# A hybrid encoder layer on one core: six feature tiles by VectorE passes, conversions ahead of the modulated input, and another order of work where the feed-forward begins

## The chip, the core and the metric

The kernel runs on one core of a Trainium2 chip. The core has TensorE (PE: matmuls into PSUM), VectorE (DVE), ScalarE (ACT), GpSimd (POOL) and SyncE (SP), which here only issues loads. The metric is the device time of one execution in microseconds (us), the median of several runs. One measurement of this kernel is the profiled execution; all rows of a trace come from that one.

## The reference, cut to what matters

One layer on x of 256 x 2048, in float32, conditioned by a vector c:

```python
c_act = silu(c)
mod = c_act @ mod_w + mod_b                          # 2048 x 12288
sh_m, sc_m, g_m, sh_f, sc_f, g_f = split(mod, 6)
h = x * (1 + sc_m) + sh_m
y = attention(h @ w_qkv + b_qkv) @ w_o + b_o          # 32 heads of 64, 8 key heads, a band of 128, a sink
x = layer_norm(2**0.25 * x + (1 + g_m) * y) 
h = x * (1 + sc_f) + sh_f
y = square(relu(h @ w1 + b1)) @ w2 + b2               # 2048 -> 8192 -> 2048
x = layer_norm(2**0.25 * x + (1 + g_f) * y)
```

## The kernel before, in words

**Three products for one.** Each float32 operand is split into a rounded high half and a low half (what is left), and a product is the sum of high by high, high by low and low by high: three matmuls (`mm3`, L554 to L556; the feed-forward's own are L1045 to L1047, L1069 and L1070). The high half of a weight is a ScalarE conversion (`wh`, L288), the low half a VectorE subtraction (`wl`, L259).

**The stream of loads.** All weights come as 1 MB loads of 128 x 2048 (`raw`, L243), issued by SyncE in the order in which `S.plan` listed them, each as soon as a buffer is free. There are eight buffers in the first stage, five after it. A load is either a weight, which needs two conversions and two subtractions of 128 x 1024, or a piece of `mod_w`.

**The modulation, in two ways.** c times a piece of `mod_w` can be made by TensorE (`Mod.step`, L343: sixteen small matmuls per load, called product loads here), whose result is copied by ScalarE (L372) and turned to columns by one small matmul (`columns`, L423), or by VectorE (`Col.step`, L383): one pass over the whole load with c spread over the rows (`cb`, made by `spread`, L139), which gives one column. For the attention's scale and shift there is one group per feature tile of 128, two loads each. The table MIXP says which way: before, tiles 4, 8 and 12 go by VectorE passes, the other thirteen by TensorE. For the feed-forward there are four groups of four tiles, and FFP says how many tiles of each go by TensorE: 0, 4, 2 and 2.

**The units.** The first stage runs over twelve units. Each takes one load of `w_qkv`, that is four pairs (tile of 128 features, a third of the first 1536 outputs), of six matmuls of 128 x 512 each; in between come the feature loads (`S.vecs(1)`, letter g of the string `steps`) and `modulated(k)` (letter m): the turn to columns, x * scale + shift as a high half on ScalarE (L582) and a low half on VectorE (L583, L584). The bias of q, k and v is split into halves by `bias_rows` and added by a matmul at the end (L204). Before the units come dummy matmuls (`idle`, L647), twenty, six and six, that keep TensorE at work while the first loads arrive.

**Attention and its output.** The remaining q, k, v weights, the scores, softmax and output projection are woven by a written order of slots (`for n in range(OUT_AT + 16)`), with loads of the gates and of the feed-forward's modulation between them (SLOT_FILL). The last slot, `project` with `last` set, finishes the 128 rows of t = 0 first, and then those of t = 1; each is followed by the norm: `add_gated`, `norm_scalars` and `normed`.

**The handover.** After that, before, `ff_columns(0)` makes the first columns, and `S.vecs(4)` takes four loads of group 2. Then `ff_input(0)` transposes the normed tile (L975), modulates it (L981 to L989), and the feed-forward's first matmuls (L1045) begin with the weights `w1a`. Loads of groups 2 and 3 are spread over the first of the sixteen `w1a` steps (W1_FILL).

**Order.** The instructions of an engine run in a fixed order. A scheduler chooses it from what is written; `keep_in_program_order` and `S.pin` hold some of them in the written order.

## Time and profile before

| | us |
|---|---|
| median of 3 runs (lowest, highest) | 1123.53 (1122.96, 1123.92) |
| the profiled execution, its own time | 1121.65 |
| its span, first to last instruction | 1119.9 |
| TensorE busy | 1077.6 (96%) |
| VectorE busy | 747.6 (67%) |
| ScalarE busy | 527.0 (47%) |

The view of the stages gives the busy time of each engine in a stretch of the span. The list of waits says for whom an engine waited. A row of the timeline has the start in us, the duration in us, the engine, the line, the operation and what it writes and reads, with the count of instructions merged into it and, in brackets, the idle time before. A TensorE matmul of float32 operands shows as two records. A row of the groups has the busy time, the mean in ns of one, and the idle time before. In the view of one loading line, "to landing" is the time from issue to arrival.

### The profile page before, as it was taken

To read this page: it belongs to the slowest core of one execution; us is meant where nothing else is said; L and a number is where in the kernel's file an instruction comes from. 1 tells how busy PE (TensorE), PEld (TensorE's weight loads), DVE (VectorE), ACT (ScalarE), POOL (GpSimd) and SP (SyncE) were. 2 spreads that over 40 slices of the span, in tenths; PEclk is the share of its full clock that TensorE was granted. 3 is DMA by queue.
4 is the path that set the end of the run, shared out by engine and by line. 5 is a ranking of instruction groups with operands and counts; after the bars stand their busy time and mean duration, and the time that the engine had idled before them with its cause. 6 is when DMAs were issued, how large, how long until landed. Compare 5 with 4: busy or idle time off the path is not lost.

```text
span 1119.9 us, 16590 instructions
## 1 busy us (share of the span) xinstructions
PE 1077.6 (96%) x6712; PEld 886.7 (79%) x6712; DVE 747.6 (67%) x1086; ACT 527.0 (47%) x817; POOL 20.4 (2%) x40
## 2 busy tenths in 40 slices
PE   8888899999999799999999999999999999999995
PEld 5666676677778599988888888888888888888884
DVE  2455497889549875765577877766665656665576
ACT  2233357788753455654345543334444334444340
POOL 1000000000000000000000000000000000000001
PEclk9999999999999899999999999999999999999998
DMA  9999978888597878455678787876555555557521
GB/s 376 400 404 403 420 293 334 304 321 309 191 391 286 329 277 320 176 188 192 224 277 299 257 291 266 310 286 222 183 186 192 195 188 188 188 188 263 188 75 75
DMA packets 43797, 292.77 MB, mean 261 GB/s; under 512 B 5020, under 2 KB 5180, under 8 KB 9928
## 3 DMA queue, kind: packets, MB, share of 16 engines
q1 hardware_dynamic: 40400, 281.83, 67.5%
q0 software_dynamic: 2432, 8.41, 2.2%
q10 hardware_dynamic: 888, 1.48, 0.4%
q8 instruction: 52, 0.85, 0.3%
q14 instruction: 25, 0.20, 0.0%
HBM read 289.58 MB, written 2.11 MB: 260 GB/s over the span
## 4 chain that ended last, share of the span: by engine, by line
PE 89%; DVE 6%; ACT 2%; DMA 2%; issue 1%; DVEq 0%; ACTq 0%; SPq 0%
PE pa L1069 16%; PE pa L554 16%; PE pa L555 16%; PE pa L556 15%; PE pa L1070 8%; PE pm L343 4%; PE pa L1045 3%; PE pa L1046 3%; PE pa L1047 3%; DVE wl L259 2%; PE pa L735 1%; PE pa L793 1%; PE pt L777 1%; ACT wh L288 1%; DVE raw L383 1%
## 5 line engine op out<-in xcount | busy, mean ns | idle before, releaser
L259 DVE TENSOR_TENSOR wl<-raw,wh 128x1024 fp32r<-128x1024 f32 x332 | 403.1, 1222 | 232.6 <-ACT wh L288 229.3
L288 ACT CAST wh<-raw 128x1024 fp32r<-128x1024 f32 x332 | 346.4, 1051 | 410.5 <-PE pa L556 212.7
L555 PE MATMUL pa<-wl,g 128*128 128x512 f32 x816 | 320.9, 393 | 4.8 <-DVE wl L259 4.8
L554 PE MATMUL pa<-wh,g 128*128 128x512 f32 x816 | 316.5, 397 | 7.9 <-ACT wh L288 7.0
L556 PE MATMUL pa<-wh,g 128*128 128x512 f32 x816 | 318.8, 391 | 0.0
L1069 PE MATMUL pa<-g,wh 128*128 128x512 f32 x768 | 271.6, 399 | 0.0
L1070 PE MATMUL pa<-g,wl 128*128 128x256 f32 x768 | 215.7, 281 | 0.0
L554 PEld LDWEIGHTS pa<-wh,g 128*128 128x128 f32 x816 | 151.7, 188 | 48.6 <-ACT wh L288 11.3
L555 PEld LDWEIGHTS pa<-wl,g 128*128 128x128 f32 x816 | 153.5, 188 | 39.3 <-DVE wl L259 6.4
L556 PEld LDWEIGHTS pa<-wh,g 128*128 128x128 f32 x816 | 153.5, 188 | 33.1 <-issue 1.2
L1069 PEld LDWEIGHTS pa<-g,wh 128*128 128x128 f32 x768 | 144.3, 188 | 36.2 <-issue 0.2
L1070 PEld LDWEIGHTS pa<-g,wl 128*128 128x128 f32 x768 | 145.1, 189 | 0.1
L383 DVE CUSTOM_DVE_ANT_0 raw<-raw,cb 128x2048 f32<-128x2048 f32 x46 | 104.8, 2283 | 8.5 <-DMA raw<-in_mod 8.3
L1045 PE MATMUL pa<-g,wh 128*128 128x256 f32 x256 | 73.2, 287 | 0.0
L1046 PE MATMUL pa<-g,wh 128*128 128x256 f32 x256 | 72.9, 285 | 0.0
L1047 PE MATMUL pa<-g,wl 128*128 128x256 f32 x256 | 72.5, 283 | 0.0
L343 PE MATMUL pm<-raw,cact 128*32 128x128 f32 (+1 forms) x1344 | 54.6, 301 | 0.0
L343 PEld LDWEIGHTS pm<-raw,cact 128*32 128x32 f32 x1344 | 36.2, 111 | 18.6 <-issue 13.5
L1045 PEld LDWEIGHTS pa<-g,wh 128*128 128x128 f32 x256 | 49.1, 192 | 1.4 <-issue 0.9
L1046 PEld LDWEIGHTS pa<-g,wh 128*128 128x128 f32 x256 | 49.2, 192 | 0.5 <-DVE g L989 0.4
L1047 PEld LDWEIGHTS pa<-g,wl 128*128 128x128 f32 x256 | 49.2, 192 | 0.0
L436 DVE TENSOR_TENSOR modm<-pt,pack 128x2 f32<-128x2 f32 x13 | 2.1, 161 | 62.8 <-PE pt L423 62.7
(183 smaller groups left out, 697.3 us busy)
## 6 DMA issues: line engine op xcount, KB each, us to landing
raw<-in_mod SPq DMA_DIRECT2D x96, 1024.0 KB, 7.5
raw<-in_w SPq DMA_DIRECT2D x64, 1024.0 KB, 4.9
raw<-in_w1b SPq DMA_DIRECT2D x48, 1024.0 KB, 5.0
raw<-in_wqkv SPq DMA_DIRECT2D x24, 1024.0 KB, 8.3
raw<-in_wo SPq DMA_DIRECT2D x16, 1024.0 KB, 7.2
raw<-in_w1a SPq DMA_DIRECT2D x16, 1024.0 KB, 7.3
g<-in_x SPq DMA_DIRECT2D x4, 512.0 KB, 7.4
gb<-in_lnrow POOLq DMA_DIRECT2D x8, 256.0 KB, 5.7
```

The costliest lines, as they stand in the source:

```text
L259: self.pinned(nc.vector.tensor_sub(l, r, f32(self.hs[n])))
L288: self.pinned(nc.scalar.copy(h, s))
L343: i = nc.tensor.matmul(self.ps[32 * j:32 * j + 32, :w], lhsT[j] if type(lhsT) is list else lhsT, rhs[j], start=self.first, stop=stop)
L383: S.pinned(nc.vector.tensor_tensor_reduce(out=raw, in0=raw, in1=cb, scale=1.0, scalar=0.0, op0=OP.mult, op1=OP.add, accum_out=self.dst))
L554: nc.tensor.matmul(ps, xh, wh, start=start, stop=False)
L555: nc.tensor.matmul(ps, xh, wl, start=False, stop=False)
L556: S.prev = nc.tensor.matmul(ps, xl, wh, start=False, stop=stop).ins
L1045: nc.tensor.matmul(o, wh(w, 128), hh, start=new, stop=False)
L1046: nc.tensor.matmul(o, wh(w, 128), hl, start=False, stop=False)
L1047: nc.tensor.matmul(o, wl(w, 128), hh, start=False, stop=end)
L1069: nc.tensor.matmul(ps, wh(k, 128), hb, start=k == 0, stop=False)
L1070: nc.tensor.matmul(ps[:, :256], wl(k, 128), hb[:, :256], start=False, stop=k == NK - 1)
```

## The change

- MIXP: tiles 6, 10 and 14 go by VectorE passes too, so six tiles do. FFP: the feed-forward's groups have 0, 4, 4 and 0 tiles by TensorE; the number of product loads stays the same.
- The dummy matmuls multiply ones, made by VectorE alone, where they multiplied GpSimd's identity; there are 12, 5, 2 and 4 of them.
- The bias rows are loaded at the start, by GpSimd's queue, and the mask is made there; the bias split comes after unit 4, `spread` after unit 1, the rotary tables in units 5 to 9.
- The string of a unit gets a letter p, `S.pump(0)`: conversions of weights that have come, ahead of the unit's last `modulated`.
- In the last slot, the feed-forward's loads (four feature loads and the first weights) are written ahead of the norm of t = 1; `ff_columns(0)` comes in slot 19. The warming of the square root's table waits for the last softmax.

```diff
-MIXP = tuple(int(k not in (4, 8, 12)) for k in range(16))
+MIXP = tuple(int(k < 4 or k % 2) for k in range(16))
 FFG = (4, 4, 4, 4)
-FFP = (0, 4, 2, 2)
+FFP = (0, 4, 4, 0)
...
-    identr = cst.tile([128, 128], F32R, name="identr")
-    nc.vector.tensor_copy(identr, ident)
+    onesr = g4(F32R)[:, :128]
+    nc.vector.memset(ones := g4()[:, :128], 1.0)
+    nc.vector.tensor_copy(onesr, ones)
...
-            nc.scalar.dma_start(raw[p:p + m, :512], src.rearrange("o (m n) -> (o m) n", m=m))
+            nc.gpsimd.dma_start(raw[p:p + m, :512], src.rearrange("o (m n) -> (o m) n", m=m))
...
-        nc.vector.tensor_copy(hl, raw[:, :512])
-        nc.vector.tensor_sub(hl[32:32 + m], raw[32:32 + m, :512], f32(hl[32:32 + m]))
-        nc.scalar.copy(sel, one)
+        def split():
+            nc.vector.tensor_copy(hl, raw[:, :512])
+            nc.vector.tensor_sub(hl[32:32 + m], raw[32:32 + m, :512], f32(hl[32:32 + m]))
+            nc.scalar.copy(sel, one)
...
     load_x(0)
+    split_bias, bq = bias_rows(a["bqkv"], QKV)
+    msk = masks()
     S.pin = True
-    idle(20)
+    idle(12)
     S.vecs(1)
-    idle(6)
+    idle(5)
     S.vecs(1)
+    idle(2)
     modulated(0)
-    idle(6)
+    idle(4)
...
-        if n == 1:
-            steps = "ugugmugug"
+        if n == 0:
+            steps = "ugugmupu"
+        elif n == 1:
+            steps = "ugugmugugp"
         else:
-            steps = ["uuuu", "ugugumu", "ugugumgug"][len(ms)]
+            steps = ["uuuu", "ugugpumu", "ugugumgugp"][len(ms)]
...
+            elif x == "p":
+                S.pump(0)
...
-        if n == 0:
+        if n == 1:
             spread()
-            bq = bias_rows(a["bqkv"], QKV)
-        if n == 1:
-            msk = masks()
-        if 3 <= n < 8:
+        if n == 4:
+            split_bias()
+        if 5 <= n < 10:
             next(tables)
...
+        if n == 15:
+            warm = sml.tile([128, 4], F32, name="warm")
+            nc.scalar.activation(warm, rs, AF.Sqrt)
...
                 if t == 0:
                     yield
+                else:
+                    for _ in range(2 * len(js)):
+                        S.done(False)
+                    S.stop, S.behind, S.pin = 0, False, True
+                    S.nh = S.nl = 2
+                    S.pump(4, 2 * S.im + 2)
+                    S.nh, S.nl, S.pin = NHIGH, NLOW, False
                 add_gated(pss[t], t, c, g1, st)
...
-            for _ in range(2 * len(js)):
-                S.done(False)
...
-        if n == 16:
-            warm = sml.tile([128, 4], F32, name="warm")
-            nc.scalar.activation(warm, sums_of[0], AF.Sqrt)
...
+        if n == 19:
+            ff_columns(0)
...
-    S.behind = False
-    ff_columns(0)
-    S.stop = 0
-    S.vecs(4)
```

The order of instructions shows what this moves. ScalarE, the last three units; `mrow` is a copied product, `modm` marks the high half of a modulated tile, `wh` a converted weight half. Before:

```order
L372 COPY mrow<-pm 128x128
L288 CAST wh<-raw 128x1024 x2
L582 ACTIVATE g_1034<-g_824,modm 128x256
L372 COPY mrow<-pm 128x128
L582 ACTIVATE g_1034<-g_824,modm 128x256
L288 CAST wh<-raw 128x1024 x2
L372 COPY mrow<-pm 128x128
L582 ACTIVATE g_1034<-g_824,modm 128x256
L288 CAST wh<-raw 128x1024 x2
```

And in the changed kernel:

```order
L375 COPY mrow<-pm 128x128
L291 CAST wh<-raw 128x1024 x2
L585 ACTIVATE g_954<-g_772,modm 128x256
L291 CAST wh<-raw 128x1024 x2
L585 ACTIVATE g_954<-g_772,modm 128x256
L375 COPY mrow<-pm 128x128
L291 CAST wh<-raw 128x1024 x2
L585 ACTIVATE g_954<-g_772,modm 128x256
```

Before, each pair of conversions stands behind the modulated tile of its unit. Now tile 14 has no copy (it goes by VectorE), and conversions stand ahead of a modulated tile in each unit.

TensorE, from the end of the last projection on; `pm` is a product load's result, `pt` a transpose, L1045 and L1053 the feed-forward's matmuls. Before:

```order
L343 MATMUL pm<-raw,cact 32x128 x48
L975 MATMUL pt<-ident,g_2500 128x128 x8
L1045 MATMUL pa<-g_3505,wh 128x256
L343 MATMUL pm<-raw,cact 32x128 x13
L1046 MATMUL pa<-g_3505,wh 128x256
L1047 MATMUL pa<-g_3505,wl 128x256
L343 MATMUL pm<-raw,cact 32x128 x3
L1045 MATMUL pa<-g_3505,wh 128x256 x2
L1046 MATMUL pa<-g_3505,wh 128x256
L1047 MATMUL pa<-g_3505,wl 128x256
```

And in the changed kernel:

```order
L346 MATMUL pm<-raw,cact 32x256 x40
L983 MATMUL pt<-ident,g_2391 128x128 x8
L1053 MATMUL pa<-g_3411,wh 128x256
L1054 MATMUL pa<-g_3411,wh 128x256
L1053 MATMUL pa<-g_3411,wh 128x256
L1054 MATMUL pa<-g_3411,wh 128x256
L433 MATMUL pt<-ident,mrow 128x128
L1055 MATMUL pa<-g_3411,wl 128x256
L1053 MATMUL pa<-g_3411,wh 128x256
L433 MATMUL pt<-ident,mrow 128x128
L346 MATMUL pm<-raw,cact 32x256 x8
L1054 MATMUL pa<-g_3411,wh 128x256
```

Five product loads (40 matmuls) now stand ahead of the transposes, where three stood (48 matmuls, each half as wide), and a sixth stands behind the first six feed-forward matmuls.

SyncE's loads around the first feed-forward weights, with the engines that each waits for (the names of the queues apart, DVE or PE is the engine that frees the buffer). Before:

```order
L243 DMA raw<-in_mod 128x2048 [waits DMAHW0_49,DVE_49]
L243 DMA raw<-in_mod 128x2048 [waits DMAHW3_49,DVE_49]
L243 DMA raw<-in_mod 128x2048 [waits DMAHW4_49,DVE_49]
L243 DMA raw<-in_mod 128x2048 [waits DMAHW5_49,DMAHW2_49,DVE_49]
L243 DMA raw<-in_mod 128x2048 [waits DVE_49]
L243 DMA raw<-in_w1a 128x2048 [waits DMAHW6_49,DVE_49]
L243 DMA raw<-in_mod 128x2048 [waits DVE_49]
L243 DMA raw<-in_w1a 128x2048 [waits DMAHW4_49,DVE_49]
```

And in the changed kernel:

```order
L246 DMA raw<-in_mod 128x2048 [waits DMAHW6_49,DVE_49]
L246 DMA raw<-in_mod 128x2048 [waits DMAHW1_49,DVE_49]
L246 DMA raw<-in_mod 128x2048 [waits DMAHW2_49,DVE_49]
L246 DMA raw<-in_mod 128x2048 [waits DMAHW3_49,DVE_49]
L246 DMA raw<-in_mod 128x2048 [waits DMAHW4_49,DVE_49]
L246 DMA raw<-in_w1a 128x2048 [waits DMAHW5_49,PE_49]
L246 DMA raw<-in_mod 128x2048 [waits DMAHW6_49,PE_49]
L246 DMA raw<-in_w1a 128x2048 [waits DMAHW7_49,PE_49]
L246 DMA raw<-in_mod 128x2048 [waits DMAHW0_49,PE_49]
```

The load of the first `w1a` weights waited for VectorE before; it waits for TensorE now, as do the next four.

More of the change, by code (lines that the diff above doesn't have):

```diff
@@ L830, in normed @@
         if t:
[L831 removed]
+            tc.keep_in_program_order(nc.scalar.activation(z, z, AF.Identity, scale=rstd, bias=sc[2]))
         else:
[L833 removed]
+            tc.keep_in_program_order(nc.vector.tensor_scalar(z, z, mv[:, 0:1], rstd, op0=OP.subtract, op1=OP.mult))
     def project(js, c):
@@ L889, in project_0, with ff_columns @@
             nc.vector.scalar_tensor_tensor(z, z, ALPHA, y, op0=OP.mult, op1=OP.add)
+    a2 = cst.tile([128, NK], F32, name="a2")
+    b2 = cst.tile([128, NK], F32, name="b2")
+    def ff_columns(g):
+        m_ff[g].columns()
+        s = slice(4 * g, 4 * g + 4)
+        scf, shf = modf[:, 0], modf[:, 1]
+        nc.vector.tensor_mul(a2[:, s], lnT[:, 0, s], scf[:, s])
+        nc.vector.tensor_mul(b2[:, s], lnT[:, 1, s], scf[:, s])
+        nc.vector.tensor_add(b2[:, s], b2[:, s], shf[:, s])
     S.nh, S.nl = NHIGH, NLOW
```

17 lines of the change are left out of this document (2 added, 15 removed).

## The prediction

> **What bounds the kernel now.** First the page: the span, the busiest engine and the load rate in forty slices of 28 us.
>
> ```profile
> span 1119.9 us, 16590 instructions
> PE 1077.6 (96%) x6712; PEld 886.7 (79%) x6712; DVE 747.6 (67%) x1086; ACT 527.0 (47%) x817; POOL 20.4 (2%) x40
> GB/s 376 400 404 403 420 293 334 304 321 309 191 391 286 329 277 320 176 188 192 224 277 299 257 291 266 310 286 222 183 186 192 195 188 188 188 188 263 188 75 75
> ```
>
> TensorE is busy 96%, so only the 42 us in which it is not, and work taken off it, can give time. Loads run at 400 to 420 GB/s in the first five slices alone. Next the busy time by stage (stretch, length, then busy us of PE, PEld, DVE, ACT, POOL, clock, DMA share, GB/s); I cut at the first projection matmul, at the end of the first twelve units, at the end of the attention output, and where TensorE is last seen waiting.
>
> ```profile
> 17.70:141.80 124.10, 108.70 (x1122) 79.30 (x1126) 61.30 (x100) 40.27 (x64) 0.00 (x0) 0.99 1.00 407
> 141.80:375.00 233.20, 231.25 (x1490) 173.16 (x1482) 187.60 (x351) 152.46 (x331) 3.86 (x7) 1.00 0.79 299
> 375.00:388.60 13.60, 5.88 (x44) 3.78 (x44) 10.88 (x28) 8.05 (x14) 0.00 (x0) 0.62 0.99 398
> 388.60:1107.40 718.80, 718.80 (x3966) 620.97 (x3963) 477.28 (x584) 321.96 (x403) 9.74 (x16) 1.00 0.62 222
> 1107.40:1119.90 12.50, 0.09 (x1) 0.00 (x0) 8.55 (x16) 0.92 (x2) 1.74 (x1) 0.69 0.22 84
> ```
>
> TensorE idles 15.4 us in the twelve units, 7.7 us where the feed-forward begins, 12.5 us at the very end, and nowhere else by more than 2 us. The end is the same program before and after. So two places decide: the units, and the 13.6 us handover. What TensorE waited for (total, times, longest):
>
> ```profile
> PE pa L554 <- ACT wh L288: 7.0, 10, 1.0
> PE pa L555 <- DVE wl L259: 4.8, 4, 2.0
> PE pt L975 <- DVE g L833: 4.7, 1, 4.7
> PE pa L647 <- DVE identr L116: 4.1, 1, 4.1
> PE pt L975 <- ACT g L831: 3.1, 1, 3.1
> ```
>
> No load is in that list, though the DMA engines are full (share 1.00) in the units. The weights of the last unit show why: issue and landing from the view of the loading line, then ScalarE's conversion and the last bias matmuls.
>
> ```profile
> L243 SPq DMA_DIRECT2D raw<-in_wqkv x1: 384/384/384, 113.7 to 113.7; - x1
> DMA to landing us min/median/max: 10.2/10.2/10.2
> 133.46 1.98 ACT L288 CAST wh<-raw 128x1024 fp32r<-128x1024 f32 x2
> 141.24 0.45 PE pa L204 x2
> ```
>
> They landed at 123.9 and were first used at 133.46: the loads are 9.6 us ahead. In the units the chain through TensorE, ScalarE and VectorE is the bound, with the loads close behind.
>
> **Term 1, the start: 4.1 us earlier.** Rows of the start, and of the second feature load.
>
> ```profile
> 0.81 0.06 DVE L118 MEMSET eps<- 128x1 f32 x1 [0.81 <-PEq L1230]
> 3.49 0.56 DVE L116 CAST identr<-ident 128x128 fp32r<-128x128 f32 x1
> 4.11 7.38 PE L647 MATMUL pa<-identr 128*128 128x512 f32 x20 [4.11 <-DVE identr L116]
> 14.02 1.08 PE L343 MATMUL pm<-raw,cact 128*32 128x128 f32 x32
> L243 SPq DMA_DIRECT2D raw<-in_mod x1: 424/424/424, 1.7 to 1.7; - x1
> DMA to landing us min/median/max: 8.2/8.2/8.2
> ```
>
> The idle matmuls no longer wait for GpSimd's identity: a memset and a 0.56 us cast on VectorE, from 0.81, release them at about 1.6. Twelve at 7.38/20 = 0.37 us end near 6.0 (6.7 at the slow clock of the first dozen). The second feature load lands at 1.7 + 8.2 = 9.9; before, its product began at 14.02, behind the dummies, and now it can begin at 9.9. What follows is the same chain, so the first projection matmul comes about 4.1 us earlier. If fewer dummies leave the clock slow, some 1 us of this goes.
>
> **Term 2, the units.** Six feature loads (tiles 6, 10 and 14) go from TensorE to VectorE.
>
> ```profile
> L343 PE MATMUL pm<-raw,cact 128*32 128x128 f32 x768 | 26.4, 279 | 0.0
> L423 PE MATMUL pt<-both,mrow 128*128 128x2 f32 x24 | 4.2, 245 | 3.0 <-ACT mrow L372 2.9
> L383 DVE CUSTOM_DVE_ANT_0 raw<-raw,cb 128x2048 f32<-128x2048 f32 x6 | 13.5, 2285 | 0.0
> ```
>
> 24 loads cost TensorE 26.4 us, so six cost 6.6; three of twelve turns (4.2 us) cost 1.05. Together with the start, even if all 15.4 us of waits remain, the chain ends at 141.7 - 4.1 - 6.6 - 1.05 = 130.0. The conversions put ahead of the modulated input and the bias split put off can only take from those waits; I count on none of that, because now the loads bind. From 17.7 to 123.9 they came at 407 GB/s on average; without their breaks, which came when buffers were not freed, at the 420 of the fifth slice, the last unit's weights land 106.2 x (1 - 407/420) = 3.3 us earlier, at 120.6. From their conversion to the last bias matmul it took 141.7 - 133.5 = 8.2 us, so the end is 128.9 by the loads. Between 128.9 and 130.0 I take 129.5: **12.2 us earlier**, the start included. Bounds: 13.3 (conversion and matmuls a little faster) and 9 (waits grow).
>
> The Trainium skill, "DMA: Bandwidth & Descriptors", section "Where 436 GB/s comes from", says that for loads from HBM the HBM side binds, at some 358 GB/s. By it these 43.2 MB would land 14.5 us later than at 407, at 138.4, and the whole change would bring 3 us. The trace disagrees, with 400 to 420 in four slices.
>
> The extra passes add 6 x 2.285 = 13.7 us to VectorE's 61.3 in 124.1, some 75 of 116: the cover is its idle time. What queues behind a pass is the low half of the next weights, and TensorE waits for that; uncovered, each tile's pair (4.6 us) could push it back by some 2 us, 6 to 8 in all.
>
> A wait also has an after-effect.
>
> ```profile
> 40.62 0.79 PE L555 MATMUL pa<-wl,g 128*128 128x512 f32 x1 [2.01 <-DVE wl L259]
> 41.21 0.63 PE L556 MATMUL pa<-wh,g 128*128 128x512 f32 x1
> L556 PE MATMUL pa<-wh,g 128*128 128x512 f32 x816 | 318.8, 391 | 0.0
> ```
>
> After a wait of 2.01 us matmuls took 0.63, where the mean of all is 0.39. VectorE kept TensorE waiting there because the bias split, now put off, stood in its queue.
>
> The Trainium skill, "TensorE: Matmul & The Clock Gate", section "HAM oscillation", lets the clock fall only after a gap of over 3.4 us. The trace is stricter; by the page the short waits for loads to come would be harmless, by the row one in some units could cost up to 2 us, which the range takes in.
>
> The stage to 375.0 keeps TensorE at 231.25 of 233.2. It loses its lead in loads, but asks for 299 GB/s of 420, so I price that at 0, up to 2 us.
>
> **Term 3, the handover.** T is the end of the last projection matmul, 372.1 before. Rows of TensorE, VectorE, ScalarE and SyncE, and a load that has the queue to itself:
>
> ```profile
> 372.17 2.83 PE L343 MATMUL pm<-raw,cact 128*32 128x128 f32 x96
> 379.65 0.69 PE L975 MATMUL pt<-ident,g 128*128 128x128 f32 x2 [4.66 <-DVE g L833]
> 383.39 1.54 PE L975 MATMUL pt<-ident,g 128*128 128x128 f32 x6 [3.05 <-ACT g L831]
> 374.97 2.28 DVE L383 CUSTOM_DVE_ANT_0 raw<-raw,cb 128x2048 f32<-128x2048 f32 x1
> 362.28 0.33 SPq L243 DMA_DIRECT2D raw<-in_w1a  x1
> 370.24 2.00 ACT L288 CAST wh<-raw 128x1024 fp32r<-128x1024 f32 x2 [10.50 <-DMA raw<-in_w1a]
> L243 SPq DMA_DIRECT2D raw<-in_w1a x1: 328/328/328, 401.3 to 401.3; - x1
> DMA to landing us min/median/max: 5.0/5.0/5.0
> ```
>
> Before, VectorE did a 2.28 us pass and weight halves between the norm's small steps, and TensorE ran freely only from 388.6, T + 16.5. Now no pass stands there: group 2 is all products, and the norm's steps follow one another, so by their order the transposes are ready before the weights; that they are is the least certain part of this term and sets its lower bound. What is late next is a load. Five product loads fill all five buffers, and TensorE takes them only after T, at 2.83/3 = 0.94 each; SyncE can issue the first feed-forward weights at T + 1.1 (before: 362.28, T - 9.8), and they land at T + 6.1 (5.0 alone). The next load, 1 MB at 420 GB/s or 2.5 us later, is a product that stands ahead of nearly all feed-forward matmuls on TensorE: landing T + 8.6, done T + 9.7. From there TensorE is free: the second weights land at T + 11.1, and 42 matmuls of the first remain, at five per 0.6 us:
>
> ```profile
> 389.94 0.28 PE L1045 MATMUL pa<-g,wh 128*128 128x256 f32 x1
> 390.54 0.28 PE L1047 MATMUL pa<-g,wl 128*128 128x256 f32 x1
> ```
>
> that is 5.0 us, to T + 14.7. So 16.5 - 9.7 = 6.8 us; three product loads that came later are done (2.8); one that now comes before T takes back 0.9; a slow clock, as the 0.62 of that stretch, may take 1: **7.7 us**, with 3 and 10 as bounds.
>
> The square root's table load moves to an earlier place on ScalarE:
>
> ```profile
> 372.26 1.28 ACT L812 ACT_TABLE_LOAD   x1
> ```
>
> It hid before, since the first root came at 375; I price it at nothing, 1.3 us if it stood in the way where it is now.
>
> The sum: 12.2 + 7.7 = 19.9. The profiled execution took 1121.65 us, 1.75 beyond its span, and would take 1101.75; the median of the runs is 1.88 higher, so the forecast is **1103.6**.
>
> **The rivals.** *The handover gives nothing* (0.13): the first weights, issued 11 us later than before, or the product behind them, land 6 us after my T + 6.1, as the 10.2 above shows that loads can when others are queued. For: the order on SyncE. Against: the queue is then empty. Time 1103.6 + 6 = 1109.6. *VectorE becomes the bound in the units* (0.08): passes hold up the low halves, 6 to 8 us as worked out, 1110.6; against it, it idles half the stage. *Loads at the rate of the first slice, 376* (0.02): 43.2 MB take 114.9 us instead of 106.2, the end is 8.2 after 132.6, one term is gone but for 0.9, and the time 1115. *Slower* (0.05): TensorE, now waiting for loads in every unit, is granted half its clock. Its work after the start is 108.7 - 7.65 = 101 us; with a share f at half clock and 15.4 us of waits it ends at 13.6 + 101 (1 + f) + 15.4. It decides from f = 0.2, where this is 150.2, 20.7 after 129.5, and eats the gain; at f = 0.25 the time is 1129. For it: the 0.63 above. Against: one such stretch in 124 us before. That the change does not do what it says is excluded by the order of instructions.
>
> **How the numbers follow.** The forecast has 0.70. Its own range: 9 to 13.3 and 3 to 10 give 12 to 23.3 off, 1100 to 1111.5. The next two rivals fall into it, so 1099 to 1112 leaves out 0.1 to 0.15. About 0.2% (2 us) is what a measurement can tell from no change. Faster has 0.93 (forecast and three rivals), same 0.02 (several misses at once), slower 0.05.
>
> **What would show it.** First projection matmul near 13.6, waits for loads on TensorE in the units, last bias matmul near 129.5, then TensorE full until T near 361; weights issued 1 us after T and TensorE full from T + 9.7. I am wrong if the units end after 133, if the clock row shows 5 or 6 there, or if TensorE waits past T + 13.

## The result, and the profile after

The changed kernel took 1116.13 us (median of 5 runs, 1114.57 to 1117.61), the kernel before 1122.97 beside it (5 runs, 1121.1 to 1123.92). The ratio is 0.9939, with a 95% interval of 0.9923 to 0.9956: 6.8 us faster, where 19.9 were forecast. The forecast of 1103.6 and its range, 1099 to 1112, were too low: the fastest of the five runs took 1114.57.

The profiled execution took 1114.57 us, with a span of 1112.8. The stages of it (stretch, length, busy us of PE, PEld, DVE, ACT, POOL, clock, DMA share, GB/s), cut as for the kernel before: at the first projection matmul, at the last bias matmul of the units, at T, where TensorE runs freely again, and where its last work ends.

```profile
13.80:134.95 121.15, 103.14 (x924) 76.81 (x928) 73.84 (x111) 40.34 (x61) 0.00 (x0) 0.94 1.01 420
134.95:367.97 233.02, 229.48 (x1399) 170.92 (x1402) 180.69 (x348) 147.22 (x328) 3.77 (x7) 1.00 0.79 296
367.97:379.40 11.43, 9.60 (x114) 5.52 (x113) 8.31 (x22) 4.95 (x8) 0.00 (x0) 0.85 0.83 328
379.40:1100.30 720.90, 717.92 (x3866) 619.22 (x3862) 487.70 (x592) 326.11 (x409) 9.75 (x16) 1.00 0.64 227
```

Loads now run at 420 GB/s through the whole first stage, and still TensorE idles 18.0 us in it, more than the 15.4 before; its mean clock there is 0.94. In the fourth stretch it idles 3.0 us, where before it idled nowhere. The list of TensorE's waits names them (total, times, longest):

```profile
PE pa L558 <- DVE wl L262: 8.5, 5, 3.5
PE pa L557 <- ACT wh L291: 5.8, 6, 1.9
PE pa L1053 <- ACT wh L291: 4.5, 4, 2.4
PE pt L462 <- ACT mrow L460: 2.9, 1, 2.9
...
PE pm L346 <- DMA raw<-in_mod: 0.8, 2, 0.5
```

The largest sum is that for `wl`, the low halves of weights, 8.5 us (4.8 before), all of it in the units. Loads as the direct cause are 0.8 us; but ahead of its conversions ScalarE waited 11.2 us for loads of `w_qkv`, four times in the units, so a part of the waits for `wh` goes back to loads. Four pieces make up the span. The third ends at the first matmul of the fifteenth of the sixteen `w1a` weights (475.68 before, 467.62 after; the expectations below say "the last of the sixteen weights" for this mark).

| piece | before | by the prediction | after |
|---|---|---|---|
| start and units, to the last bias matmul | 141.69 | 129.5 | 134.95 |
| from there to T (with one product load more, 0.9) | 230.55 | 231.5 | 233.02 |
| T to the fifteenth `w1a` weights | 103.45 | 94.85 | 99.64 |
| from there to the end | 644.19 | 644.2 | 645.18 |
| span | 1119.9 | 1100.0 | 1112.8 |

So 5.4 us are missing in the units, 1.5 on the way to T, 4.8 in the handover and 1.0 behind it.

**Where the units lose it.** Rows of ScalarE, VectorE and TensorE in unit 6, whose modulated input is tile 10, one of the three new pass tiles, in order of time (start, duration, instruction, and in brackets the idle time before and what ended it):

```profile
76.51 2.00 ACT L291 CAST wh<-raw 128x1024 fp32r<-128x1024 f32 x2 [0.99 <-DMA raw<-in_wqkv]
...
77.59 1.22 DVE L262 TENSOR_TENSOR wl<-raw,wh 128x1024 fp32r<-128x1024 f32 x1 [1.44 <-ACT wh L291]
...
79.83 2.28 DVE L386 CUSTOM_DVE_ANT_0 raw<-raw,cb 128x2048 f32<-128x2048 f32 x1
...
82.04 2.29 DVE L386 CUSTOM_DVE_ANT_0 raw<-raw,cb 128x2048 f32<-128x2048 f32 x1
...
83.98 1.99 ACT L291 CAST wh<-raw 128x1024 fp32r<-128x1024 f32 x2 [4.97 <-DMA raw<-in_wqkv]
...
85.88 0.60 ACT L585 ACTIVATE g<-g,modm 128x256 fp32r<-128x256 f32 x1
...
86.51 0.41 DVE L586 TENSOR_SCALAR g<-g,modm 128x256 f32<-128x256 f32 x1 [1.97 <-ACT g L585]
...
88.05 2.35 DVE L262 TENSOR_TENSOR wl<-raw,wh 128x1024 fp32r<-128x1024 f32 x2
...
89.32 0.80 PE L558 MATMUL pa<-wl,g 128*128 128x512 f32 x1 [3.50 <-DVE wl L262]
89.91 0.63 PE L559 MATMUL pa<-wh,g 128*128 128x512 f32 x1
```

Both high halves of this unit's weights are ready at 78.51. One low half is made at 77.59; the other, ready to be made from 78.51, comes at 88.05. Ahead of it in VectorE's order stand the two passes, the low half of the modulated tile (L586, L587) and the first steps of the rotary tables (0.8 us, not shown); L586 waits for the modulated high half on ScalarE (85.88), and that stands behind the conversions of the next weights, put ahead of it by the letter p, which wait until 83.98 for their load. TensorE needs the low half at 85.82 and stands still for 3.50 us. Afterwards its matmuls take 0.63 us where 0.39 is the mean: the granted clock is 0.50 from 85.65 to 92.47.

**The handover.** T is 367.97, and the loads are as forecast, to 0.2 us: the first weights are issued at 369.03 (T + 1.1) and landed 4.8 us later. Rows of TensorE from there on:

```profile
367.90 4.52 PE L346 MATMUL pm<-raw,cact 128*32 128x256 f32 x80
...
375.06 0.38 PE L1053 MATMUL pa<-g,wh 128*128 128x256 f32 x1 [1.27 <-ACT wh L291]
...
377.58 1.84 PE L346 MATMUL pm<-raw,cact 128*32 128x256 f32 x16
...
430.08 0.39 PE L1053 MATMUL pa<-g,wh 128*128 128x256 f32 x1 [2.35 <-ACT wh L291]
```

The last product load takes 1.84 us instead of 0.94, and it begins at 377.58, 1.2 us after it landed (376.38): the first matmuls of the first weights stand ahead of it, which waited 1.27 and 0.45 us for their conversions and then ran at half clock. So TensorE is free at T + 11.4, not T + 9.7. And 60 us later it waits again, at the ninth weights, for 2.35 and then for 0.39 us: a wait that no step of the prediction had. Rows of VectorE and ScalarE ahead of it:

```profile
423.20 2.29 DVE L386 CUSTOM_DVE_ANT_0 raw<-raw,cb 128x2048 f32<-128x2048 f32 x1
...
425.93 1.02 ACT L989 ACTIVATE g<-pt,b,a 128x256 fp32r<-128x256 f32 x2 [4.78 <-DVE b L914]
...
429.00 1.98 ACT L291 CAST wh<-raw 128x1024 fp32r<-128x1024 f32 x2
```

The ninth weights had landed at 421.48. Their conversion stands behind the input of group 2 (L989) on ScalarE, which waits 4.78 us for the group's columns (`b`, L914); these stand behind a pass of group 3 on VectorE.

### The profile page after: what moved, and what is told of

Same layout as the page of the kernel before. It is cut to its first block, busy times and chain, and to the rows that moved or that the text cites. A ratio compares the mean times of both kernels' runs of the same rounds, so it can differ in the third digit from the quotient of the medians.

```text
span 1112.8 us, 15919 instructions
## 1 busy us (share of the span) xinstructions
PE 1071.0 (96%) x6377; PEld 880.0 (79%) x6377; DVE 761.2 (68%) x1098; ACT 522.9 (47%) x811; POOL 21.4 (2%) x42
## 3 DMA queue, kind: packets, MB, share of 16 engines
HBM read 289.58 MB, written 2.11 MB: 262 GB/s over the span
## 4 chain that ended last, share of the span: by engine, by line
PE 83%; DVE 8%; ACT 3%; DMA 3%; issue 2%; POOL 0%; SPq 0%; DVEq 0%; ACTq 0%; POOLq 0%
PE pa L1077 16%; PE pa L558 15%; PE pa L559 14%; PE pa L557 14%; PE pa L1078 8%; PE pm L346 3%; PE pa L1053 3%; DVE wl L262 3%; PE pa L1054 3%; PE pa L1055 3%; DVE raw L386 2%; DMA raw<-in_wqkv 1%; ACT wh L291 1%; PE pa L744 1%; PE pa L802 1%
## 5 line engine op out<-in xcount | busy, mean ns | idle before, releaser
L386 DVE CUSTOM_DVE_ANT_0 raw<-raw,cb 128x2048 f32<-128x2048 f32 x52 | 118.2, 2283 | 10.1 <-DMA raw<-in_mod 10.1
L1053 PE MATMUL pa<-g,wh 128*128 128x256 f32 x256 | 73.0, 288 | 4.5 <-ACT wh L291 4.5
L1053 PEld LDWEIGHTS pa<-g,wh 128*128 128x128 f32 x256 | 49.4, 194 | 5.4 <-ACT wh L291 5.4
L346 PE MATMUL pm<-raw,cact 128*32 128x128 f32 (+1 forms) x1024 | 47.0, 324 | 0.9 <-DMA raw<-in_mod 0.8
L346 PEld LDWEIGHTS pm<-raw,cact 128*32 128x32 f32 x1024 | 28.0, 112 | 19.4 <-issue 11.7
L761 ACT ACTIVATE g<-g,nm 128x256 f32<-128x256 f32 x64 | 31.8, 499 | 16.8 <-DVE nm L751 16.7
```

Of the source, the lines that this page charges most:

```text
L346: i = nc.tensor.matmul(self.ps[32 * j:32 * j + 32, :w], lhsT[j] if type(lhsT) is list else lhsT, rhs[j], start=self.first, stop=stop)
L386: S.pinned(nc.vector.tensor_tensor_reduce(out=raw, in0=raw, in1=cb, scale=1.0, scalar=0.0, op0=OP.mult, op1=OP.add, accum_out=self.dst))
L1053: nc.tensor.matmul(o, wh(w, 128), hh, start=new, stop=False)
```

## The experiments

All times are medians of 4 to 11 runs, against the kernel before on the same chip (1122.4 to 1123.2 us); the interval is that of the ratio to it.

### The low halves

Theory Q: in the in-order queues of ScalarE and VectorE the low half that TensorE needs next stands behind steps that it does not need. Its rivals are the loads, and the clock for a cause of its own.

**e1, a low half right behind its high half.** In the changed kernel a low half is written once the next high half is, or when its own unit begins.

```diff
-    if len(self.ls) < n - 1 and len(self.ls) - self.used < self.nl or ...
+    if len(self.ls) < n - (not self.pin) and len(self.ls) - self.used < self.nl or ...
```

> In the units a weight's second low half is written right behind its own high half, where the changed kernel writes it behind the next weight's first conversion. Nothing else differs. Theory Q (the in-order queues of ScalarE and VectorE hold up the low halves, and the waits halve the clock): TensorE's waits for wl in the units, 8.5 us in the changed kernel, fall below 3; the half-clock stretches, 13.65 us of the units there, fall to one of 3.4 or none; the units end near 130 instead of 134.6 and the time is about 1111.5. Rival L (the loads, or the time that TensorE itself needs, set the end): waits of about the same sum turn up on other tiles, the end stays at 134 to 135 and the time at 1116. Rival C (the half clock comes by itself and is no consequence of the waits): the waits go, the half-clock stretches stay, the end is near 132.

It took 1108.34 us, ratio 0.9864 (0.9850 to 0.9878): 7.8 less than the changed kernel by the medians. The profiled executions are 4.6 apart (here the slowest of four runs, there the fastest of five): 5.0 less in the units, 1.6 more on the way to T, where a half-clock stretch came at 202.3, 0.2 more in the handover, and 1.4 less behind it, where the edit changes nothing. The stage of its units, by the same view as above:

```profile
13.76:129.93 116.17, 102.64 (x924) 76.43 (x928) 73.46 (x110) 39.80 (x60) 0.00 (x0) 0.96 1.01 419
```

TensorE's waits in the whole of it:

```profile
PE pa L557 <- ACT wh L291: 6.4, 6, 1.8
...
PE pa L558 <- DVE wl L262: 4.3, 6, 1.9
```

And the timeline of VectorE in unit 6 and of ScalarE at the last unit's weights:

```profile
77.78 2.36 DVE L262 TENSOR_TENSOR wl<-raw,wh 128x1024 fp32r<-128x1024 f32 x2 [0.79 <-ACT wh L291]
...
80.84 2.28 DVE L386 CUSTOM_DVE_ANT_0 raw<-raw,cb 128x2048 f32<-128x2048 f32 x1
...
120.24 1.99 ACT L291 CAST wh<-raw 128x1024 fp32r<-128x1024 f32 x2
```

The units end at 129.93. TensorE idles 13.5 us instead of 18.0, and that is 4.5 of the 5.0 us; so the gain is in the waits, not in the clock, of which Q had expected more (the stretches at half clock are 10.2 us instead of 13.65, but the one that went was one in which TensorE stood still anyway); nor did the waits for `wl` fall below 3. The last weights, landed at 120.22, are converted at 120.24, those of the unit before, landed at 112.77, at 112.80, and ScalarE waits 14.5 us for loads ahead of its conversions: now the loads bind, as the prediction's term had it. In unit 6 both low halves are now made ahead of the passes, which are the same and as long.

**e2, without the letter p.**

```diff
-            steps = "ugugmupu"
+            steps = "ugugmuu"
...
-            steps = ["uuuu", "ugugpumu", "ugugumgugp"][len(ms)]
+            steps = ["uuuu", "ugugumu", "ugugumgug"][len(ms)]
```

> The changed kernel without the letter p: no conversions of weights ahead of the modulated input, all else as changed. Theory Q: ScalarE no longer waits for the next weights' load ahead of the high half of tiles 6, 10 and 14, so the high half and with it the low half come 1 to 2 us earlier there, but the second low half still stands behind the passes; the units end at 132 to 134 instead of 134.6, time 1113.5 to 1116. Rival P (the letter p is a gain, since it puts conversions earlier): waits for wh grow by a conversion and a modulated half in each of the ten units, about 1 us each, the end is near 140 and the time 1121.

1120.91 us, 0.9978 (0.9967 to 0.9988); the units end at 144.02. The rival was right: the waits for `wh` are 12.1 us, where they were 5.8. Q's picture was incomplete. Rows of ScalarE and VectorE in unit 6:

```profile
79.69 2.00 ACT L291 CAST wh<-raw 128x1024 fp32r<-128x1024 f32 x2
...
83.01 2.29 DVE L386 CUSTOM_DVE_ANT_0 raw<-raw,cb 128x2048 f32<-128x2048 f32 x1
...
88.39 0.41 DVE L586 TENSOR_SCALAR g<-g,modm 128x256 f32<-128x256 f32 x1 [0.67 <-ACT g L585]
...
89.93 3.49 DVE L262 TENSOR_TENSOR wl<-raw,wh 128x1024 fp32r<-128x1024 f32 x3
```

Both high halves of this unit's weights are ready at 81.69, but now both low halves, not only the second, stand behind the passes and the modulated tile 10. From its list of waits:

```profile
PE pa L558 <- DVE wl L262: 10.3, 4, 8.7
```

One wait has become 8.7 us long. The letter p is worth some 5 us to this change: it is the smaller of two evils.

**e4, without p and with the low halves at once.** Both edits above.

> The changed kernel without the letter p and with each low half written right behind its own high half. Theory Q: both causes of held-up halves are gone; at best the loads bind, W11's weights land near 120 and the units end at 128.9 to 130.5, time 1110 to 1112. If the letter p is needed (rival P), waits for wh take the place of those for wl and the end is at 134 or later, time 1116 or more.

1119.67 us, 0.9965 (0.9953 to 0.9977), units to 143.98: nearly the same as e2. In unit 9 the edit acts (the first low half comes 0.7 us behind its high half, 6.6 in e2), but not in unit 6: the high halves are ready at 81.87, the first low half again comes at 90.11, behind the passes, and TensorE waits 8.72 us for it. The waits for `wl` are 10.3 us as in e2, those for `wh` 11.4, so the time is the rival's, though one wait did not take the place of the other. Why the order in unit 6 stayed the traces do not show; what they show is that without p the edit of e1 gains nothing.

**e3, three tiles by passes instead of six.**

```diff
-MIXP = tuple(int(k < 4 or k % 2) for k in range(16))
+MIXP = tuple(int(k not in (4, 8, 12)) for k in range(16))
```

> The changed kernel with three feature tiles by VectorE passes as before (4, 8, 12) instead of six. TensorE gets the 6.6 us of product loads and 1.05 us of turns back. Theory Q (the passes are what holds up the low halves): of the 8.5 us of waits for wl and the 6.8 us that the half clock takes, about as much goes as TensorE gains work, and the units end at 133 to 136, the time is 1115 to 1118, so that the three further tiles bring nothing in the units. Rival (the passes cost nothing and TensorE's work counts in full): the end is near 142, the time 1124.

1114.81 us, 0.9931 (0.9917 to 0.9945), units to 134.54, where the changed kernel had 134.95; four kernels with the same units (the changed one, e8, e9 and e13) end them at 134.38 to 135.22. Their stage:

```profile
13.89:134.54 120.65, 108.57 (x1122) 79.67 (x1126) 60.83 (x99) 40.75 (x63) 0.00 (x0) 0.97 1.01 419
```

TensorE is busy 5.4 us longer (not 7.65, since in the changed kernel more of the work runs at half clock) and waits 5.9 less (12.1). So the three further tiles, 7.65 us of work by the prediction, bring nothing in the changed kernel: what they take off TensorE comes back as waits.

**e11, three tiles with the low halves at once.** The edits of e3 and e1.

> Three feature tiles by passes as before, with each low half right behind its high half. It tells what the three further tiles are worth once the low halves are not held up. If TensorE's 7.65 us count there: the units end 4 to 7.65 us later than with six tiles and the same order of halves (129.9), at 134 to 137.6, time 1112 to 1116. If the loads or the waits for high halves set the end: 130 to 131, time 1108 to 1109.

1109.33 us, 0.9894 (0.9871 to 0.9917), units to 131.78, 1.85 later than in e1. Their stage:

```profile
13.96:131.78 117.82, 107.05 (x1122) 77.88 (x1126) 60.60 (x98) 40.17 (x63) 0.00 (x0) 1.00 1.01 419
```

Of the 7.65 us only 1.85 is left, because with six tiles the loads bind and with three they do not: here ScalarE waits for no load ahead of a conversion, the last weights, landed at 120.02, are converted at 122.78, and TensorE works without a wait from 108 to the end of the units. It has more work but waits 10.8 us instead of 13.5, and none of it runs at half clock. In the time the two kernels cannot be told apart: this one's runs went from 1108.2 to 1116.7, with a mean clock from 0.995 down to 0.988, on which more at the end.

**e12, the kernel before with the low halves at once.** The edit of e1 in the kernel before.

> The kernel before, with each low half right behind its high half in the units. Its waits for wl there are 4.8 us in four places, with one half-clock stretch. Theory Q, if the held-up halves are old: 2 to 5 us faster than before, 1118 to 1121. If they are the change's own making (letter p and six tiles): within 1.5 us of before, 1121.5 to 1124.

1117.62 us, 0.9956 (0.9942 to 0.9969): 5 us by the ratio, of which its profiled execution, the slowest of its runs, shows 2.2. The held-up halves are older than the change; with it, by the medians, there is more to win from them (7.8). Rows of the kernel before, ahead of the wait of 2.01 us that the prediction shows:

```profile
26.25 1.98 ACT L288 CAST wh<-raw 128x1024 fp32r<-128x1024 f32 x2
...
36.56 0.16 DVE L436 TENSOR_TENSOR modm<-pt,pack 128x2 f32<-128x2 f32 x1 [8.03 <-PE pt L423]
...
39.34 1.23 DVE L259 TENSOR_TENSOR wl<-raw,wh 128x1024 fp32r<-128x1024 f32 x1
```

The low half could have been made from 28.23 and was made at 39.34. The bias split took 1.1 us of that on VectorE; for 8.03 us VectorE stood idle ahead of a step for the modulated tile, with the low half behind it in its order.

**e5, dummy matmuls in the two longest waits of the units.**

```diff
+FILL = {6: 20, 10: 8}
...
+            if i == 2:
+                for _ in range(FILL.get(n, 0)):
+                    tc.keep_in_program_order(nc.tensor.matmul(sums[p][0], zer, wh(i), start=False, stop=False))
```

> The changed kernel with dummy matmuls (zeros by a weight half, added to a sum that is open, so that nothing in the result changes) where TensorE waits longest: 20 in unit 6, ahead of its third pair, and 8 in unit 10. At 0.23 us each they fill 4.6 of the 5.4 us and 1.8 of the 2.3 us that TensorE idles there; the halves that it waits for come no earlier. Theory Q (a wait of some 2 us makes the clock fall to half for 3.4 us or a multiple): the half-clock stretches behind those two waits, 10.2 us together, go, the units end 4 to 5 us earlier, near 130, and the time is near 1111.5, although more is computed. Rival C (the half clock has another cause): the stretches stay, the end is at 135 to 136 and the time at 1116 to 1117.

1116.50 us, 0.9946 (0.9932 to 0.9959), units to 136.64. It tells little. The dummies of unit 10 ran at 125.67, 7 us behind the wait that they were meant for, which stayed at 2.26 us; those of unit 6 (4.8 us) left a wait of 2.56 there, since TensorE, at full clock where it had been at half, came to them earlier. Half-clock stretches followed both waits. So neither theory falls by it, though the time is C's.

### The two halves of the change

**e6, the units' part alone; e7, the handover's part alone.** In both, the diff of the change is split between `MIXP`, the start, the bias rows and `steps` on one side, and `FFP`, `warm`, `normed`, `project` and `ff_columns` on the other.

> The kernel before with the first half of the change alone (start, six feature tiles, letter p, bias split), without the other order where the feed-forward begins. By the terms of the prediction, 12.2 us: 1110.8. By what the trace of the changed kernel shows (units end 6.7 us earlier, 2 us of it given back before the feed-forward): 1117 to 1119.

> The kernel before with the second half of the change alone: the feed-forward's loads ahead of the norm of t = 1, the first columns in slot 19, group 2 all by TensorE and group 3 all by VectorE, the table's warming. By the prediction's term, 7.7 us: 1115.3. By the trace of the changed kernel (from the end of the projection to the last of the sixteen feed-forward weights 99.6 us instead of 103.5, less 0.9 for the product load that comes before it): 1119 to 1120.

e6 took 1118.16 us, 0.9966 (0.9953 to 0.9978); e7 1120.97, 0.9982 (0.9973 to 0.9991). Against the runs beside them (1122.56) that is 4.4 and 1.6 us, together 6.0, near the 6.8 of the whole: the halves do not disturb each other much. In e7 TensorE waited 3.01 us at the first `w1a` matmul, the weights landing 6.6 us after their issue instead of the 5.0 that were counted: 1.6 us of what the rival "the handover gives nothing" had named.

### The wait at the ninth weights

**e8, the passes of group 3 planned earlier.**

```diff
-    W1_FILL = [1, 1, 1, 0, 0, 2, 0, 3, 0, ...
+    W1_FILL = [1, 1, 1, 0, 0, 3, 0, 4, 0, ...
```

> The changed kernel with the eight pass loads of group 3 planned earlier by one or two places (W1_FILL 3 and 4 at the sixth and eighth weight instead of 2 and 3, none left for the ninth), so that the last two passes are written ahead of the columns of group 2. Theory Q: the last two passes no longer stand ahead of those columns on VectorE, ScalarE's conversion of the ninth weights no longer waits behind the group's input, and the wait of 2.35 and 0.39 us at 427.7 goes with the half-clock stretch of 3.4 us behind it: 4.4 us, time 1111.5 to 1113. Rival L (loads bind there: the sixth to eighth weights have 2.7 to 4.3 us to spare and come 2.5 us later each): waits of 1 to 4 us on those weights take its place, time 1115 to 1117.

1117.06 us, 0.9951 (0.9939 to 0.9963): nothing. The wait went from the ninth weights to the eighth, and grew. Rows of ScalarE and TensorE there:

```profile
422.27 1.02 ACT L989 ACTIVATE g<-pt,b,a 128x256 fp32r<-128x256 f32 x2 [0.25 <-DVE b L914]
...
425.34 1.98 ACT L291 CAST wh<-raw 128x1024 fp32r<-128x1024 f32 x2
...
426.43 0.58 PE L1053 MATMUL pa<-g,wh 128*128 128x256 f32 x1 [4.05 <-ACT wh L291]
```

The eighth weights had landed at 418.0; their conversion stood behind the input of group 2 (L989) on ScalarE. So the wait is as long as rival L had it, but the loads are not its cause.

**e9, the input of group 2 ahead of the sixth weights.**

```diff
-        if n in (1, 7, 9):
+        if n in (1, 5, 9):
```

> The changed kernel with the columns and the input of group 2 made ahead of the sixth feed-forward weights instead of the eighth (their product loads, all by TensorE now, are done at 379). Theory Q: these columns stood on VectorE behind passes of group 3, ScalarE's input of group 2 behind the columns, and the conversion of the ninth weights behind that input; with the columns ahead of the passes the wait of 2.74 us at 428 and the half-clock stretch behind it (1.7 us) go: from the end of the projection to the last of the sixteen weights 95 to 96 us instead of 99.6, time 1111.5 to 1112.5. Rival W (the wait only moves: the passes now come behind the columns, and the input of group 3 waits for them): one wait of 2 to 4 us elsewhere before the last of the sixteen weights, 98 us or more, time 1115 to 1116.

1113.83 us, 0.9921 (0.9908 to 0.9934), from T to the mark 98.8 instead of 99.6; against the changed kernel's 0.9939 (0.9923 to 0.9956) that is no clear gain. Rival W was nearer: the input is done by 417, and the ninth weights' conversion now stands behind another step, a copy of sums (L1059) that waits for TensorE. Rows of both:

```profile
427.73 0.58 ACT L1059 COPY g<-pa 128x512 f32<-128x512 f32 x1 [2.05 <-PE pa L1055]
428.21 4.83 ACT L291 CAST wh<-raw 128x1024 fp32r<-128x1024 f32 x5
...
429.31 0.38 PE L1053 MATMUL pa<-g,wh 128*128 128x256 f32 x1 [1.62 <-ACT wh L291]
```

**e10, e1 and e9 together.**

> The changed kernel with both edits: a low half right behind its high half in the units, and the input of group 2 ahead of the sixth weights. If the two held-up queues are all that was missing of the forecast, and are independent: 1108.3 less 4.4, that is 1104; the forecast was 1103.6. If a wait takes the place of the second: 1108.

1108.64 us, 0.9875 (0.9860 to 0.9889): no faster than e1 alone. T to the mark is 96.9 instead of 99.9, but the rest takes 646.2 instead of 643.8. Of these 2.4 us, 0.9 are matmuls that start late for `wl` between 680 and 710 (1.9 in all, 1.0 in e1), and 1.5 is the second block of the hidden layer, which takes 90.8 us in fourteen of the profiled executions and 89.4 in the other four, e1 among them, without a wait that shows. Why it does is open.

### The clock

**e13 to e16, dummy matmuls in the waits behind the units.** Ten ahead of the gate's transposes, five ahead of the first `w1a` matmul and ten ahead of the ninth weights' first matmul: in the changed kernel (e13), in e1 (e14), in e10 (e15) and in e11 (e16).

```diff
+    def fill(ps, n):
+        for _ in range(n):
+            tc.keep_in_program_order(nc.tensor.matmul(
+                ps, fil, fil[:, None, :].to_broadcast([128, 4, 128]), start=True, stop=True))
...
             nc.scalar.copy(r, m.ps[:, :256])
+            fill(pt, 10)
...
             ps = opened[fq, fp]
+            if fp == 0 and n in (0, 8):
+                fill(ps, 5 if n == 0 else 10)
```

> The changed kernel with dummy matmuls (into a bank that the next matmul overwrites) at the three places behind the units where TensorE waits: ten ahead of the gate's transposes (wait 2.94 us at 203), five ahead of the first feed-forward matmul (1.27 and 0.45 at 374), ten ahead of the ninth weights' first matmul (2.35 and 0.39 at 428). They fill 2.3, 1.2 and 2.3 us of the waits; what TensorE waits for comes no earlier. Theory G (the clock is set in a fixed grid of stretches of 3.41 us: one in which TensorE idles for half or more makes the next one run at half clock): no half-clock stretch behind these places any more; 3.4 us less than the profiled execution of the changed kernel, which had two of them, 4 us less in the median, whose runs also had one at 207: 1112 to 1113. Rival C (the clock has another cause, such as the load on TensorE before): the stretches stay, 1116.

> The same dummies in the kernel with each low half right behind its high half. That kernel's profiled execution had half-clock stretches at 202.3, 373.0 and 427.6, behind the units. Theory G: all three go, 5.1 us less than its 1108.3: 1103 to 1104.5. Rival C: 1108.

> The same dummies with both edits, the low halves and the input of group 2 ahead of the sixth weights. Theory G: two or three half-clock stretches go, 1103.5 to 1105.5 where it was 1108.6. Whether the early input of group 2 brings anything, now that its wait no longer costs clock: 0 to 1.5 us against the run without it.

> The same dummies with three feature tiles by passes and each low half right behind its high half. Its profiled execution had one half-clock stretch only, at 426.7, its runs 1108.2 to 1116.7. Theory G: 1.7 us less than the best of these or more, 1105 to 1107; against the run with six tiles and the same dummies it tells what three further tiles are worth: 1 to 2 us by the ends of the units, 131.8 and 129.9.

The view of the stages, cut at the clock's own grid of 3.41 us (busy TensorE is the first number behind the length, the clock the third from the end). In e1 2.51 of the 2.94 us of wait ahead of the gate's transposes fall into one stretch:

```profile
198.88:202.28 3.40, 0.89 (x8) 0.89 (x9) 3.40 (x9) 1.96 (x5) 0.00 (x0) 1.00 0.63 186
202.29:205.69 3.40, 3.40 (x18) 1.94 (x18) 2.92 (x3) 2.12 (x3) 0.00 (x0) 0.50 0.98 393
```

In the changed kernel the grid cuts the same wait in two, and at the ninth weights it does not:

```profile
201.71:205.11 3.40, 1.76 (x20) 0.71 (x18) 3.27 (x5) 2.72 (x6) 0.00 (x0) 1.00 0.53 219
205.12:208.52 3.40, 2.11 (x18) 1.70 (x20) 3.37 (x7) 2.44 (x7) 0.00 (x0) 1.00 0.93 318
208.53:211.93 3.40, 3.40 (x24) 2.25 (x21) 3.19 (x8) 1.69 (x3) 0.00 (x0) 1.00 0.97 342
...
426.99:430.39 3.40, 1.04 (x9) 0.83 (x7) 3.34 (x11) 2.29 (x4) 0.00 (x0) 1.00 1.01 410
430.40:433.80 3.40, 3.01 (x15) 2.77 (x14) 3.29 (x4) 3.40 (x6) 0.00 (x0) 0.50 0.85 284
```

With 0.89 or 1.04 us of work in a stretch the next one runs at 0.50; with 1.76 and 2.11 it does not. Where dummies fill the waits, at the gate's transposes in e14 (e1 with dummies) and at the ninth weights in e13:

```profile
197.99:201.39 3.40, 2.98 (x16) 2.04 (x13) 3.40 (x7) 2.72 (x7) 0.00 (x0) 1.00 0.49 118
201.41:204.81 3.40, 3.40 (x31) 2.37 (x31) 3.37 (x5) 2.13 (x4) 0.00 (x0) 1.00 0.90 376
...
427.51:430.91 3.40, 3.40 (x28) 3.31 (x28) 3.40 (x6) 2.22 (x5) 0.00 (x0) 1.00 1.01 378
430.92:434.32 3.40, 3.40 (x24) 3.07 (x23) 3.33 (x8) 3.40 (x5) 0.00 (x0) 1.00 1.00 369
```

At these two places, eight in the four kernels, no half-clock stretch is left; without the dummies the same four kernels had one at five of the eight. And no dummy brought forward what was waited for: the waits make the half clock, theory G. At the first `w1a` weights one stayed in each (two in e14), since there the wait went to the product load: 2.6 us, and 3.9 in e16.

The time followed only in part: none of the four lies where G had put it, and e14 is at rival C's 1108. e13: 1114.24 us, 0.9924 (0.9911 to 0.9938), 1.9 less than the changed kernel though the intervals overlap, and its runs lie within 0.8 us where the changed kernel's lie within 3.0. e14: 1108.12, 0.9873 (0.9858 to 0.9888), the same as e1; e15: 1108.63, 0.9875 (0.9861 to 0.9889), the same as e10. In e13 and e14 a wait of 1.6 us for ScalarE turned up at 271 and 266 (0.4 in e15 and e16), and 2.6 us in front of the product load. e16: 1112.88, 0.9916 (0.9903 to 0.9928), 4.8 more than e14: with its units at 133.48 (131.78 in e11, without the half-clock stretch that came at 97.74 here) and the longer wait for the product load it speaks for six tiles, where e1 and e11 could not be told apart, and by more than the 1 to 2 us that were expected. So the cause of the half clock is shown, and what its removal is worth in time is not.

The fastest are e14, e1, e15 and e10, 1108.1 to 1108.6 and not to be told apart: 14 to 15 us below the kernel before and 8 below the changed one.

## Why the prediction was wrong, point by point

- **What bounds the units.** "In the units the chain through TensorE, ScalarE and VectorE is the bound, with the loads close behind": right for the kernel before.
- **Term 1, the start.** Right: the first projection matmul came at 13.80, 13.6 forecast, and the smaller number of dummies cost nothing.
- **Term 2, the units: this step failed.** Its load half was right: 420 GB/s without breaks, the last weights landed at 120.03 (120.6 forecast). Its other half, "even if all 15.4 us of waits remain", took the waits for a constant that the change could only lower. They rose to 18.0, and three stretches of work at half clock came with them, where before there was one. Of the 5.4 us that are missing, 2.6 are these waits, 2.1 are TensorE's busy time (103.1 us, where 108.7 - 7.65 = 101.0 had been counted), and the rest is the choice of 129.5 over 130.0 and the start. The cause had been named ("what queues behind a pass is the low half of the next weights"), priced at 6 to 8 us and given 0.08, because VectorE idles half the stage. That was the wrong argument: it was busy 73.8 of 121 us in the trace of after, and held up TensorE for 8.5 us. e1 is the proof: with 73.5 us of the same VectorE steps in another order, the units end at 129.93, within 0.5 us of the forecast, and the loads bind. The rival's price was 1110.6 for the whole; the units' part of it, 5.4 us, is near its 6 to 8. The trace of before already held the counterexample, in the very wait of 2.01 us that the prediction shows and puts down to the bias split (rows at e12).
- **The stage to T, priced at 0 to 2.** 1.5 us went there beyond the product load that had been counted: the wait for `mrow` grew from 1.79 to 2.94, and one of 0.5 (L729, for VectorE) is new. It was said that this stage loses its lead in loads; what grew was ScalarE's queue, not a load: the copy stands behind a step (L776) that itself waited 0.68 us for VectorE.
- **Term 3, the handover.** Its first half was right to 0.2 us: issue, landing, the product load behind. Its size was off by 4.8 us: TensorE was free 1.7 us later, because the last product load began 1.0 us later than forecast, behind matmuls of the first weights that waited and ran at half clock, and took 1.84 us for 0.94; a wait of 2.74 us at the ninth weights, in the steps that had been taken for equal, was new; and half a stretch of 3.41 us, 1.7, came behind that. Together 6.1, of which 1 us had been allowed for a slow clock; that is about what is missing. The wait comes from the change of FFP: group 3, all by passes now, puts them into the stretch where the input of group 2 and the ninth weights' conversion queue. Taking one of these out of the way (e8, e9) showed the next one in the queue; none of them alone gives the time back. The root's table load, priced at nothing, was right: it comes at 304.34, where TensorE does not wait.
- **The rest of the program**, taken for equal, was 1.0 us longer, 0.9 of it in three places (687, 693 and 715) where matmuls by low halves start late, each too short for the list of waits.
- **The rivals.** "The handover gives nothing", with weights that land late, did not occur (4.8 us from issue to landing), nor did loads at 376 GB/s; nor did the half clock with a share of 0.2 and more: 13.65 us of 121 are 0.11.

The Trainium skill's limit of 358 GB/s for loads from HBM ("DMA: Bandwidth & Descriptors", section "Where 436 GB/s comes from"; it is given there as one core's half of a stack's 716) does not hold for this kernel: 420 over 121 us, on one core.

## What to carry to other kernels

An engine that idles two fifths of the time can still be the bound of a stage: ask not how busy it is, but what stands ahead of the one step that the next engine waits for, in the engine's written order. When work is moved from the bounding engine to such a one, look at each place where it lands for a step that is due soon and ready, and put that one first; here one term in the rule that writes the low halves was worth, by the medians, as much as the whole change. And a wait that is taken away by moving its step shows the next step in the same queue, so its whole length is rarely gained.

## What the chip showed that was not expected

TensorE's clock is decided in a fixed grid of stretches of 3.41 us, which lies differently in each execution. Counted over the 18 profiled executions, between 14 and 1085 us and from the matmul records: after a full-clock stretch with 1.9 us or more of idle time the next one ran at half clock in 54 of 54 cases; with 1.3 to 1.9 us in 19 of 47; with less in one (1.12 us, e12). So a wait of some 2 us costs up to another 1.7 us, half a stretch, if it falls within one stretch, and nothing where the grid cuts it as above. Steps of about 1.7 us between the runs of one program fit this, but only one execution of each kernel was profiled, so for the other runs (a stretch at 207 in those of the changed kernel, as e13's expectation has it) it is an inference: the changed kernel's five lie at 1114.6 to 1114.7, 1116.1 and 1117.5 to 1117.6, and the six of e11 at 1108.2 to 1109.7 with a mean clock of 0.994 to 0.995, and at 1113.7 and 1116.7 with 0.988.

The Trainium skill, "TensorE: Matmul & The Clock Gate", section "What's actually happening", has the window of 3413 ns and that it runs freely: the traces agree (3.41 us, another phase in each). By the same section, and by "HAM oscillation", it takes an idle window, or a gap of over 3.4 us, to lose the clock; the traces show a bound of about half of that.
